# A hybrid attention block: the mixed values of two query tiles share one PSUM bank

## The chip, the cores and the metric

The kernel runs on one core of a Trainium2 chip. The core has a matrix engine (TensorE, PE in the profile), a vector engine (VectorE, DVE), a scalar engine (ScalarE, ACT), GpSimd (POOL), and queues that issue transfers (SyncE, SP). The metric is the device time of one execution in microseconds, as the median of several runs. The kernel before took 745.53 us (743.57 to 746.62, three runs).

## The reference

One encoder block on 1024 tokens of width 1024. The normalised input is projected once, and the parts feed attention, a gated spatial mix and the merge gates. Cut to what matters here:

```
q, k, v, gate_a, u_in, v_in, gate_b, g_merge = split(rmsnorm(x) @ w_in)
q, k = rope(rmsnorm(q)), rope(rmsnorm(k))      # 8 query heads, 2 key heads, 64 wide
p = softmax(q @ k.T / 8)                       # one row of 1024 weights per query
attn = (p @ v) * silu(gate_a)
gm = gelu(u_in) * v_mix * silu(gate_b)         # v_mix: spatial mix of layernorm(gelu(v_in))
y = sigmoid(g0) * (attn @ w_proj_attn) + sigmoid(g1) * (gm @ w_proj_gmlp)
out = rmsnorm(x + y @ w_out)
```

## The kernel before

Numbers that need more precision than the matrix engine's fast type gives are split into a high and a low part, and three products of parts make one product (`mm3`, L171). After the projections of k, v and q the kernel is in its attention stage, the part that the change edits.

**Scores.** Attention runs over 64 "heads": 4 groups `j` of two query heads, 8 query tiles `qt` of 128 tokens, 2 heads `h`; head number n is 16j + 2qt + h. For each, `scores` (L545) makes four matmuls of 512 columns into one of three PSUM tiles of 1024 columns (L550, L551), DVE takes the negated row maximum (`nm`, L553), ACT the exponential (`P`, L557), DVE the reciprocal of the sum (`ri`, L560), ACT the high part of the 16-bit weights (`p`, L563) and DVE their low part (L564). SP issues a transposing transfer of both parts (L567) into `T`, of which there are two buffers, one per pair (j, qt). Of `P` and `p` there are two buffers each for heads up to 11, and three from head 12 on.

**Mix.** `mix` (L569) multiplies the transposed weights of both heads of a pair (j, qt) with the values `vS`: 16 matmuls of 256 columns into the first half of the one PSUM bank `o`. The values' high parts sit in output partitions 0 to 63 and their low parts in 64 to 127, so ACT copies partitions 64 to 127 to SBUF (L578, tile `o2`, its own buffer) and DVE adds it to the other half, once for each head, 128 columns each (L582), into `og`. There are 32 mixes.

**Fills.** Between the heads stand 24 half projections of 512 tokens, the "fills": `u` (gelu), `gb` and `ga` (silu). Each is 24 matmuls of 512 columns (`z_mm`, L485) into the one PSUM bank `z`, which DVE evicts with a multiplication (`uw` L511, `gb..w` and `ga..w` L494), followed by two or three more steps on DVE and ACT and a product on POOL or DVE. Their SBUF tiles come from one set of four rotating tiles of 512 columns, `t2`. Their weights are loaded by SP into four raw buffers (`wraw`, L120), the high part is made by ACT (`wh`, L110) and the low part by POOL (`wl`, L116), which sets the raw buffer free.

**Order.** The text writes five scores ahead, two fills as a ramp, and then for each of 32 steps two more scores, one mix and the fills that `plan` gives to that step (L584 to L620). This is only where the tiles are handed out; a scheduler of the framework then sets the order of instructions on each engine, by its own model of time, and may place an instruction ahead of others of the text when its tiles are free. On the chip each engine takes its instructions strictly in that order.

**After it.** `proj_b` (L631, eight times 24 matmuls, `yb`) overlaps the stage's end, ACT and DVE make the sums and parts of the input that the gate products need (`xf`, `xfT`, `gf`, `gk`), and the gate products (`g`, L686 on) begin. Each gate weight is scaled by a factor (`scg`) from its squares: ACT squares four blocks of it (`gsq`, L814), PE adds them over the partitions (`usg`, L669), DVE and POOL make the factor, and ACT scales the weight (`wg`, L680).

Of the kernel before, what the change touches and what calls it, by code (L numbers as in the profile page):

```python
# [9 lines left out]
F32 = mybir.dt.float32  # L10
# [3 lines left out]
ALU = mybir.AluOpType  # L14
# [16 lines left out]
def hybrid_block_kernel(  # L31
# [11 lines left out]
    act, dve, pool, pe = nc.scalar, nc.vector, nc.gpsimd, nc.tensor  # L43

    sb = ctx.enter_context(tc.tile_pool(name="sb", bufs=1))
# [7 lines left out]
    def t4(tag, name, dt=F32, shape=(P, 1024)):  # L53
        return sb.tile(list(shape), dt, tag=tag, bufs=BUFS[tag], name=name)

    def t2(name, dt=F32):
        return sb.tile([P, 512], dt, tag="t2", bufs=4, name=name)

    def t8(tag, bufs, name, dt=F32R):
        return sb.tile([P, 2, 1024], dt, tag=tag, bufs=bufs, name=name)  # L60
# [13 lines left out]
    def ps_o(name):  # L74
        return ps.tile([P, 512], F32, tag="o", bufs=1, name=name)
# [7 lines left out]
    def H(h):  # L83
        return slice(512 * h, 512 * h + 512)

    def C(c):
        return slice(128 * c, 128 * c + 128)

    def heads(ap):
        return ap.rearrange("p (h d) -> p h d", d=64)  # L90
# [87 lines left out]
    for i in range(4):  # L178
        for j in range(2):
# [12 lines left out]
            for tt in range(NT):  # L192
                o = kvb[tt // 2][:, 256 * (tt % 2):256 * (tt % 2) + 256]
# [69 lines left out]
    for h in range(2):  # L263
        pt = ps_o(f"wsum{h}")
        pe.matmul(pt, ones, wsr[h], start=True, stop=True)
        for t in (2 * h, 2 * h + 1):
            for g2 in range(2):
                rows = slice(64 * g2, 64 * g2 + 64)
                dve.scalar_tensor_tensor(
                    out=bterm[rows, t, :], in0=pt[rows, C(2 * (t % 2) + g2)], scalar=cs[rows, C_LNB + t:C_LNB + t + 1],  # L270
                    in1=bsp[rows, C(t)], op0=ALU.mult, op1=ALU.add)
# [117 lines left out]
    for tab, o in (((rtk[:, 1, H(0)], rtk[:, 1, H(1)]), 128), (tabq, 0)):  # L389
        for half in range(2):  # L390
            dve.tensor_tensor(
                out=heads(tab[half]), in0=heads(rtk[:, 0, H(half)]),
                in1=gq[:, None, o + 64 * half:o + 64 * half + 64].broadcast_to([P, 8, 64]),
                op=ALU.mult)
# [5 lines left out]
    vS = sb.tile([P, 8, 2, 128], F16, tag="vS", bufs=1, name="vS")  # L400
# [19 lines left out]
                      in1=e2[:, None, :].broadcast_to([P, 2, 64]), op=ALU.mult)  # L420
# [57 lines left out]
    for t in range(4):  # L478
        m3 = vm[:, t, :].rearrange("p (c i) -> p c i", i=128)
        dve.scalar_tensor_tensor(out=m3, in0=m3, scalar=cs[:, C_LNG + t:C_LNG + t + 1],  # L480
                                 in1=bterm[:, t:t + 1, :].broadcast_to([P, 8, 128]),
# [40 lines left out]
    og, gat = {}, {}  # L522
# [45 lines left out]

    def mix(j, qt):  # L569
        v = j // 2  # L570
        ot = ps_o(f"o{j}{qt}")
        T = T16[j, qt]
        for kt in range(8):
            for p in range(2):
                pe.matmul(ot[:, 0:256], vS[:, kt, v, :], T[:, :, 8 * p + kt, :],  # L575
                          start=(kt == 0 and p == 0), stop=(kt == 7 and p == 1))
        o2 = sb.tile([64, 256], F32, tag="o2", bufs=1, name=f"o2{j}{qt}")
        act.copy(o2, ot[64:128, 0:256])  # L578
        if qt == 0:
            og[j] = t4("og", f"og{j}")  # L580
        for h in range(2):
            dve.tensor_tensor(out=og[j][64 * h:64 * h + 64, C(qt)], in0=ot[0:64, C(h)], in1=o2[:, C(h)], op=ALU.add)  # L582

    order = ["u2", "a0", "u0", "b1", "u1", "u3", "a1", "b0", "b2", "b3", "a2", "a3"]  # L584
    halves = [(o[0], int(o[1]), h) for o in order for h in range(2)]
    ramp = 2
# [25 lines left out]
    for n in range(32):  # L612
        if ramp + n in late:
            q_post(late[ramp + n], qsts[late[ramp + n]])
        for m in (2 * n + ahead, 2 * n + ahead + 1):
            if m < 64:
                scores(*hs[m])
        mix(*hs[2 * n][:2])
        for f in plan.get(n, []):
            run_fill(*f)  # L620
# [160 lines left out]
    for dt in range(8):  # L781
        proj_b(dt)
        if dt in XCS:
            j = XCS.index(dt)
# [97 lines left out]
    for step in MORDER.split():  # L882
# [13 lines left out]
        elif step[0] == "a":  # L896
            t = t8("qT", 4, f"ya{i}", F32)
# [135 lines left out]
```

## Time and profile before

| | |
|---|---|
| median of 3 runs | 745.53 us (743.57 to 746.62) |
| the profiled execution | 744.79 us |
| its span, first to last instruction | 743.0 us |
| mean granted TensorE clock | 0.988 |
| busy: PE, DVE, ACT, POOL | 712.1, 596.4, 446.8, 97.2 us |
| attention stage, mixes from first to last | 164 to 441 us |

A group of the profile names a line, an engine, the operation, what it writes and reads, the shapes, and the number of instructions; then the busy time and the mean duration of one in ns; then how long the engine stood idle just before them, and what ended most of that wait. A timeline row gives the start, the duration, and the idle time before it in brackets. Durations of neighbouring instructions overlap, so the price of one on a full engine is read from start to start.

### The profile page before, as it was taken

How to read it: one execution, taken by the hardware profiler on the slowest of the kernel's cores; microseconds unless marked ns; L12 is line 12 of the kernel's file. 1: busy time of each engine (PE TensorE's matmuls, PEld its weight loads, DVE VectorE, ACT ScalarE, POOL GpSimd, SP SyncE). 2: the span in 40 equal slices, each digit the busy share in tenths (PEclk: the TensorE clock that was granted, in tenths of full speed). 3: DMA queues.
4: the chain of work that ended last, by engine and by line, in shares of the span. 5: the costliest groups of instructions: out<-in, count | busy, mean ns of one | idle time of the engine just before them, and what ended most of it. 6: DMA issues, size and time to landing. Idle time of an engine off the chain costs nothing.

```text
span 743.0 us, 9814 instructions
## 1 busy us (share of the span) xinstructions
PE 712.1 (96%) x3561; PEld 530.1 (71%) x3561; DVE 596.4 (80%) x931; ACT 446.8 (60%) x775; POOL 97.2 (13%) x77
## 2 busy tenths in 40 slices
PE   8999999988999999999999995999999998999995
PEld 8978888766778888888878882455464555588884
DVE  5568988789798999988899999899888899934223
ACT  6646664676788898768787488555474446611101
POOL 0010242142121321232200002000000000000000
PEclk9999999989999999999999998999999999999998
DMA  8831301083769897898999800130031006241111
GB/s 309 301 100 36 114 15 42 1 142 78 136 128 181 166 179 142 162 177 157 166 234 323 183 16 1 56 128 15 18 125 57 0 1 231 109 142 68 46 58 56
DMA packets 152609, 85.47 MB, mean 115 GB/s; under 512 B 135408, under 2 KB 136048, under 8 KB 152560
## 3 DMA queue, kind: packets, MB, share of 16 engines
q1 hardware_dynamic: 152272, 84.56, 45.7%
q8 instruction: 28, 0.46, 0.3%
q10 hardware_dynamic: 288, 0.28, 0.1%
q14 instruction: 21, 0.17, 0.1%
HBM read 47.07 MB, written 4.19 MB: 69 GB/s over the span
## 4 chain that ended last, share of the span: by engine, by line
PE 81%; DVE 9%; DMA 4%; ACT 2%; issue 2%; POOL 1%; SPq 0%; POOLq 0%; DVEq 0%; ACTq 0%
PE o L575 6%; PE out L174 4%; PE out L173 4%; PE out L172 4%; DMA T<-p 3%; PE s L550 3%; PE s L551 3%; PE g L172 3%; PE g L174 3%; PE g L173 3%; PE q L172 2%; PE q L174 2%; PE v L172 2%; PE q L173 2%; PE v L173 2%; PE v L174 2%
## 5 line engine op out<-in xcount | busy, mean ns | idle before, releaser
L564 DVE SCALAR_TENSOR_TENSOR p<-P,ri,p 128x1024 f16<-128x1024 f32 x64 | 88.9, 1393 | 14.7 <-ACT p L563 14.3
L557 ACT ACTIVATE P<-s,nm 128x1024 f32<-128x1024 f32 x64 | 71.4, 1116 | 23.0 <-DVE nm L553 11.5
L553 DVE TENSOR_REDUCE nm<-s 128x1 f32<-128x1024 f32 x64 | 77.8, 1215 | 5.7 <-PE s L551 5.4
L563 ACT ACTIVATE p<-P,ri 128x1024 f16<-128x1024 f32 x64 | 72.8, 1143 | 14.7 <-DMA T<-p 11.3
L575 PE MATMUL o<-T,vS 128*128 128x256 f16 x512 | 61.8, 273 | 2.1 <-DMA T<-p 2.1
L575 PEld LDWEIGHTS <-vS 128*128 128x128 f16 x512 | 47.4, 98 | 16.0 <-issue 6.9
L550 PE MATMUL s<-kT,qT 128*128 128x512 f32 x128 | 53.0, 414 | 1.3 <-ACT P L557 1.3
L116 POOL TENSOR_TENSOR wl<-wraw,wh 128x512 fp32r<-128x512 f32 x24 | 36.0, 1504 | 111.6 <-ACT wh L110 96.2
L551 PE MATMUL s<-kT,qT 128*128 128x512 f32 x128 | 50.5, 395 | 0.0
L909 ACT ACTIVATE sq<-xr 128x1024 f32<-128x1024 f32 x7 | 7.4, 1061 | 61.5 <-DVE xr L963 61.5
L963 DVE TENSOR_TENSOR xr<-out,xr 128x1024 f32<-128x1024 f32 x7 | 8.6, 1225 | 44.0 <-PE out L174 43.9
L673 POOL TENSOR_TENSOR scg<-scg,mhalf 128x1 f32<-128x1 f32 x8 | 9.8, 1219 | 221.6 <-DVE scg L672 221.6
L110 ACT CAST wh<-wraw 128x512 fp32r<-128x512 f32 x35 | 21.5, 614 | 17.5 <-PE yb L173 7.5
L488 PE MATMUL ga<-xh,wh 128*128 128x512 f32 x64 | 26.5, 414 | 3.8 <-DVE uw L511 3.4
L550 PEld LDWEIGHTS s<-kT,qT 128*128 128x128 f32 x128 | 24.1, 188 | 6.7 <-ACT P L557 1.9
L551 PEld LDWEIGHTS s<-kT,qT 128*128 128x128 f32 x128 | 24.1, 188 | 4.9 <-issue 0.2
L488 PE MATMUL u<-xh,wh 128*128 128x512 f32 x64 | 25.6, 399 | 0.7 <-DVE ga01w L494 0.7
L490 PE MATMUL ga<-xh,wl 128*128 128x512 f32 x64 | 26.1, 407 | 0.0
L489 PE MATMUL ga<-xl,wh 128*128 128x512 f32 x64 | 26.0, 406 | 0.0
L680 ACT ACTIVATE wg<-graw,scg 128x512 f16<-128x512 f32 x16 | 11.4, 721 | 24.2 <-PE g L174 12.8
L172 PE MATMUL v<-nh,xh 128*128 128x512 f32 x64 | 25.5, 398 | 0.0
L174 PE MATMUL yb<-gmh,wl 128*128 128x512 f32 x64 | 25.5, 398 | 0.0
(557 smaller groups left out, 2158.5 us busy)
## 6 DMA issues: line engine op xcount, KB each, us to landing
wraw<-in_wall_dram SPq DMA_DIRECT2D x59, 256.0 KB, 3.2
graw<-in_wall_dram SPq DMA_DIRECT2D x16, 512.0 KB, 4.4
xraw<-in_xT_dram SPq DMA_DIRECT2D x15, 512.0 KB, 7.3
xn<-in_x_dram SPq DMA_DIRECT2D x8, 512.0 KB, 7.6
wor<-in_wall_dram SPq DMA_DIRECT2D x8, 512.0 KB, 4.9
xr<-in_x_dram SPq DMA_DIRECT2D x8, 512.0 KB, 5.1
out_dram<-xr SPq DMA_DIRECT2D x7, 512.0 KB, 2.6
T<-p SPq DMA_TRANSPOSE x64, 4.6
```

Source lines behind the costliest of these rows:

```text
L116: eng_lo.tensor_tensor(out=lo, in0=raw, in1=hi if hi.dtype == F16 else hi.bitcast(F32), op=ALU.subtract)
L172: pe.matmul(o, ah, bh, start=start, stop=False)
L173: pe.matmul(o, ah, bl, start=False, stop=False)
L174: pe.matmul(o, al, bh, start=False, stop=stop)
L488: pe.matmul(o, wh[:, C(dt % 4)], xh[dt][:, H(h)], start=(dt == 0), stop=False)
L550: pe.matmul(sp[:, H(hf)], qs, kT[:, 2 * v, H(hf)], start=True, stop=False)
L551: pe.matmul(sp[:, H(hf)], qs, kT[:, 2 * v + 1, H(hf)], start=False, stop=True)
L553: dve.tensor_reduce(out=nm, in_=sp, axis=AX.X, op=ALU.max, negate=True)
L557: act.activation(Pt, sp, AF.Exp, bias=nm, accum_out=rsum)
L563: act.activation(hi, Pt, AF.Copy, scale=ri)
L564: dve.scalar_tensor_tensor(out=lo, in0=Pt, scalar=ri, in1=hi, op0=ALU.mult, op1=ALU.subtract)
L575: pe.matmul(ot[:, 0:256], vS[:, kt, v, :], T[:, :, 8 * p + kt, :], start=(kt == 0 and p == 0), stop=(kt == 7 and p == 1))
```

## The change

The mixes of an even query tile and the odd one behind it share the bank: the even one writes columns 0 to 255, the odd one 256 to 511. Only after the odd one are they evicted, by one copy of 512 columns on ACT and two additions of 256 columns on DVE (two pieces of 128, picked by a stepped access), where two copies of 256 and four additions of 128 were. The copy's target is now one of the `t2` tiles that the fills use; the buffer `o2` is gone.

```
     def mix(j, qt):
         v = j // 2
-        ot = ps_o(f"o{j}{qt}")
+        if qt % 2 == 0:
+            ots[j] = ps_o(f"o{j}{qt}")
+        ot = ots[j][:, 256 * (qt % 2):256 * (qt % 2) + 256]
         T = T16[j, qt]
         for kt in range(8):
             for p in range(2):
-                pe.matmul(ot[:, 0:256], vS[:, kt, v, :], T[:, :, 8 * p + kt, :],
+                pe.matmul(ot, vS[:, kt, v, :], T[:, :, 8 * p + kt, :],
                           start=(kt == 0 and p == 0), stop=(kt == 7 and p == 1))
-        o2 = sb.tile([64, 256], F32, tag="o2", bufs=1, name=f"o2{j}{qt}")
-        act.copy(o2, ot[64:128, 0:256])
         if qt == 0:
             og[j] = t4("og", f"og{j}")
+        if qt % 2 == 0:
+            return
+        o2 = t2(f"o2{j}{qt}")[0:64, :]
+        act.copy(o2, ots[j][64:128, :])
+        o4, l4 = (t.rearrange("p (k h t) -> p k h t", k=2, h=2) for t in (ots[j], o2))
         for h in range(2):
-            dve.tensor_tensor(out=og[j][64 * h:64 * h + 64, C(qt)], in0=ot[0:64, C(h)], in1=o2[:, C(h)], op=ALU.add)
+            dve.tensor_tensor(
+                out=og[j][64 * h:64 * h + 64, 128 * qt - 128:128 * qt + 128].rearrange("p (k t) -> p k t", k=2),
+                in0=o4[0:64, :, h, :], in1=l4[:, :, h, :], op=ALU.add)
+    ots = {}
```

The line numbers behind this function grow by 8 in the changed kernel. The scheduler sets a new order on every engine from the first mixes on. Three places of it follow.

DVE before, around the eviction of the second `gb` half (gb11w). `p` is a head's low part, `nm` its maximum, `ri` its reciprocal, `og` a mix's two additions.

```order
L582 TENSOR_TENSOR og_1659<-o_2012,o_2029 64x128 x2
L560 RECIPROCAL ri_1987<-ri_1987 128x1
L564 SCALAR_TENSOR_TENSOR p_1951<-P_1945,ri_1948,p_1951 128x1024
L553 TENSOR_REDUCE nm_2038<-s_2033 128x1
L564 SCALAR_TENSOR_TENSOR p_1990<-P_1984,ri_1987,p_1990 128x1024
L560 RECIPROCAL ri_2004<-ri_2004 128x1
L494 TENSOR_TENSOR gb11w<-gb_2297,rB 128x512
L553 TENSOR_REDUCE nm_2055<-s_2050 128x1
L560 RECIPROCAL ri_2043<-ri_2043 128x1
L564 SCALAR_TENSOR_TENSOR p_2007<-P_2001,ri_2004,p_2007 128x1024
```

The same eviction on DVE in the changed kernel, with what follows it.

```order
L553 TENSOR_REDUCE nm_2703<-s_2698 128x1
L560 RECIPROCAL ri_2673<-ri_2673 128x1
L494 TENSOR_TENSOR gb11w<-gb_2277,rB 128x512
L564 SCALAR_TENSOR_TENSOR p_2676<-P_2670,ri_2673,p_2676 128x1024
L497 SCALAR_TENSOR_TENSOR gb11t<-gb11t,gb11w 128x512
L511 TENSOR_TENSOR uw_2398<-u_2373,rB 128x512
L275 SCALAR_TENSOR_TENSOR ut_2400<-ut_2400,uw_2398 128x512
L587 TENSOR_TENSOR og_2360<-o_2343,o_2457 64x256 x2
L277 SCALAR_TENSOR_TENSOR ut_2400<-ut_2400,uw_2398 128x512
L511 TENSOR_TENSOR uw_2538<-u_2513,rB 128x512
L275 SCALAR_TENSOR_TENSOR ut_2540<-ut_2540,uw_2538 128x512
```

Before, gb11w stood among heads 14 to 18 (`nm_2055` is head 18's maximum); now it stands behind head 31's maximum (`nm_2703`), and two of the four halves of u1 and u3 follow with hardly a head between them.

SP before, from the transposes of pair 10 (heads 20 and 21) to those of pair 12; `wraw` is a weight's load.

```order
L567 DMA_TRANSPOSE T_2122<-p_2119 128x16x128
L120 DMA wraw_3126<-in_wall_dram 128x512
L567 DMA_TRANSPOSE T_2122<-p_2341 128x16x128
L120 DMA wraw_3362<-in_wall_dram 128x512
L567 DMA_TRANSPOSE T_2361<-p_2358 128x16x128
L567 DMA_TRANSPOSE T_2361<-p_2443 128x16x128
L567 DMA_TRANSPOSE T_2463<-p_2460 128x16x128
L567 DMA_TRANSPOSE T_2463<-p_2499 128x16x128
```

SP in the changed kernel, the same pairs.

```order
L567 DMA_TRANSPOSE T_2103<-p_2100 128x16x128
L567 DMA_TRANSPOSE T_2103<-p_2321 128x16x128
L567 DMA_TRANSPOSE T_2341<-p_2338 128x16x128
L567 DMA_TRANSPOSE T_2341<-p_2419 128x16x128
L120 DMA wraw_2607<-in_wall_dram 128x512
L120 DMA wraw_2838<-in_wall_dram 128x512
L120 DMA wraw_2844<-in_wall_dram 128x512
L120 DMA wraw_3075<-in_wall_dram 128x512
L120 DMA wraw_3081<-in_wall_dram 128x512
L567 DMA_TRANSPOSE T_2439<-p_2436 128x16x128
L567 DMA_TRANSPOSE T_2439<-p_2474 128x16x128
```

Before, loads stood between single transposes; now five stand in a row ahead of the transposes of pair 12 (`T_2439`, heads 24 and 25).

ACT before, at the end of the stage, from the copy of the last `proj_b` product to the first scaled gate weight.

```order
L637 COPY y_4201<-yb_4546 128x1024
L110 CAST gk<-gat_3889 128x1024
L814 ACTIVATE gsq_4733,gss_4732<-graw_4729 128x512
L110 CAST gf_4914<-gat_3889 128x1024
L110 CAST xfT_4268<-xraw_4208 128x512
L814 ACTIVATE gsq_4735,gss_4732<-graw_4729 128x512
L814 ACTIVATE gsq_4737,gss_4732<-graw_4729 128x512
L814 ACTIVATE gsq_4739,gss_4732<-graw_4729 128x512
L110 CAST xfT_4314<-xraw_4210 128x512
L680 ACTIVATE wg_4606<-graw_4578,scg_4592 128x512
```

ACT in the changed kernel, the same stretch.

```order
L645 COPY y_4121<-yb_4466 128x1024
L110 CAST gk<-gat_3820 128x1024
L110 CAST xfT_4241<-xraw_4130 128x512
L110 CAST xfT_4423<-xraw_4253 128x512
L110 CAST gf_4834<-gat_3820 128x1024
L110 CAST xfT_4241<-xraw_4132 128x512
L688 ACTIVATE wg_4526<-graw_4498,scg_4512 128x512
```

The four squares (`gsq`) that stood behind the copy have moved ahead of it.

## The prediction

> **What bounds the kernel now.** First the page: the busy shares, then the engines' shares of the chain that ended last.
>
> ```profile
> PE 712.1 (96%) x3561; PEld 530.1 (71%) x3561; DVE 596.4 (80%) x931; ACT 446.8 (60%) x775; POOL 97.2 (13%) x77
> PE 81%; DVE 9%; DMA 4%; ACT 2%; issue 2%; POOL 1%; SPq 0%; POOLq 0%; DVEq 0%; ACTq 0%
> ```
>
> TensorE (PE) carries 81% of the chain, but busy time alone does not say that it is full, since its rows overlap. So next the stretches of time. The attention stage, which the change edits, runs from 164 to 441 us; after it come the gap before the gate products (441 to 456) and the rest.
>
> ```profile
> 164.00:240.00 76.00, 71.23 (x400) 57.28 (x399) 66.13 (x94) 56.85 (x108) 17.95 (x12) 1.00 0.71 131
> 240.00:280.00 40.00, 40.00 (x215) 32.43 (x213) 39.77 (x57) 34.86 (x63) 11.29 (x8) 1.00 0.91 177
> 280.00:441.00 161.00, 159.75 (x845) 128.86 (x844) 145.79 (x217) 118.65 (x204) 22.38 (x15) 1.00 0.83 178
> 441.00:456.00 15.00, 7.37 (x33) 5.64 (x32) 14.50 (x26) 14.70 (x31) 1.54 (x1) 0.88 0.00 1
> ```
>
> The columns are start:end, length, then busy us of PE, weight loads, DVE, ACT and POOL, the clock, the DMA share and GB/s. Two engines are full at once: PE pauses for 6 us in 277, and DVE reaches 39.77 of 40 us between 240 and 280. Between 441 and 456 PE stands for half of the time.
>
> How far PE really is from its limit is read from start to start, in a stretch of its timeline without idle time (18 matmuls of 512 columns, one mix of 16 matmuls of 256, then scores):
>
> ```profile
> 359.66 0.40 PE L488 MATMUL ga<-xh,wh 128*128 128x512 f32 x1
> ...
> 363.58 0.40 PE L551 MATMUL s<-kT,qT 128*128 128x512 f32 x1
> 363.82 1.92 PE L575 MATMUL o<-T,vS 128*128 128x256 f16 x16
> 365.49 0.48 PE L550 MATMUL s<-kT,qT 128*128 128x512 f32 x1
> 365.81 0.39 PE L551 MATMUL s<-kT,qT 128*128 128x512 f32 x1
> ```
>
> 18 starts in 4.16 us are 0.231 us each, and I use 0.2325; a mix takes 1.67 us and 0.09 more at the change of type, 1.76 us or 0.11 per matmul. The DVE's prices from start to start, in the same way, stand in these rows (maximum, a mix's two additions, a silu step, a weight's low part, a reciprocal, a head's low part; then an addition of 256 columns):
>
> ```profile
> 395.56 1.22 DVE L553 TENSOR_REDUCE nm<-s 128x1 f32<-128x1024 f32 x1
> 396.70 0.57 DVE L582 TENSOR_TENSOR og<-o,o 64x128 f32<-64x128 f32 x2
> 397.30 0.69 DVE L497 SCALAR_TENSOR_TENSOR ga30t<-ga30t,ga30w 128x512 f32<-128x512 f32 x1
> 397.91 0.68 DVE L116 TENSOR_TENSOR wl<-wraw,wh 128x512 fp32r<-128x512 f32 x1
> 398.51 0.15 DVE L560 RECIPROCAL ri<-ri 128x1 f32<-128x1 f32 x1
> 398.58 1.26 DVE L564 SCALAR_TENSOR_TENSOR p<-P,ri,p 128x1024 f16<-128x1024 f32 x1
> 399.77 0.68 DVE L494 TENSOR_TENSOR ga31w<-ga,rB 128x512 f32<-128x512 f32 x1
> ...
> 488.55 0.40 DVE L714 TENSOR_TENSOR ps<-wraw 128x256 f32<-128x256 f32 x1
> 488.87 0.68 DVE L696 TENSOR_TENSOR gb<-g1T,ga 128x512 f32<-128x512 f32 x1
> ```
>
> That is 1.14, 0.60 (two of 0.30), 0.61, 0.60, 0.07, 1.19, and 0.32 for 256 columns.
>
> **The direct saving.** The copies and additions, by form, with a 512-wide cast beside them:
>
> ```profile
> L582 DVE TENSOR_TENSOR og<-o,o 64x128 f32<-64x128 f32 x64 | 17.8, 278 | 1.7 <-ACT o L578 1.2
> L578 ACT COPY o<-o 64x256 f32<-64x256 f32 x32 | 11.9, 371 | 9.1 <-PE o L575 8.4
> L110 ACT CAST wh<-wraw 128x512 fp32r<-128x512 f32 x27 | 16.6, 613 | 12.4 <-PE yb L173 7.5 <-PE u L489 1.6 <-issue 1.4
> ```
>
> Sixteen pairs of mixes each lose two additions. On DVE a pair costs 4 x 0.30 = 1.20 us now and 2 x 0.33 = 0.66 after: 16 x 0.54 = 8.6 us. That row of 256 columns reads SBUF and the new additions read PSUM in steps; at worst two cost what four did, at best the same 0.32. On ACT two copies of 0.371 become one of about 0.61: 16 x 0.13 = 2.1 us. The Trainium skill (Perfetto Trace Analysis, Optimizing Scalar/DVE Operations) gives a fixed access overhead of about 125 ns for DVE and 51 ns for ScalarE on PSUM; by it 32 fewer additions would save an estimated 4.0 us and 16 fewer copies 0.8 us. The rows give twice that on DVE; with either, the sum below is the same but for 1 us, since only eight additions fall in the stretch that decides.
>
> None of this shortens the stage by itself. PE has the same rows, 0.2325 and 0.11 us each, and fills the stage.
>
> **What moves.** The copy's target is no longer a tile of its own but one of the four rotating 512-column tiles (t2) that the fills use too. These are handed out in the order of the text. A fill whose text stands behind a mix can no longer be placed before that mix's copy. Before, the scheduler ran fills ahead: the first u half after the ramp was evicted (uw_2213) behind head 8's low part. In the new order it is evicted (uw_2193) only behind head 19's. Attention then runs for a while with few fills, and four u halves follow in a heap.
>
> In the part before the heap PE has little to do per head and DVE much. I sum both from fixed points, the end of head 5's score matmuls at 167.00 us on PE and head 4's low part at 168.34 on DVE, to the eviction of gb11 (gb11w), which frees the only z bank for the first u half of the heap.
>
> ```profile
> 167.00 0.83 PE L575 MATMUL o<-T,vS 128*128 128x256 f16 x6
> 168.34 1.28 DVE L564 SCALAR_TENSOR_TENSOR p<-P,ri,p 128x1024 f16<-128x1024 f32 x1
> 225.29 0.67 DVE L494 TENSOR_TENSOR gb11w<-gb,rB 128x512 f32<-128x512 f32 x1
> L564 DVE SCALAR_TENSOR_TENSOR p<-P,ri,p 128x1024 f16<-128x1024 f32 x60 | 83.2, 1390 | 14.7 <-ACT p L563 14.3
> ...
> 175.23 2.53 DVE L326 TENSOR_TENSOR qtmp<-qst,tabq 128x256 f32<-128x256 f32 x4
> 178.95 1.20 DVE L329 TENSOR_TENSOR qst<-qst,tabq 128x1024 f32<-128x1024 f32 x1
> 180.07 0.57 DVE L582 TENSOR_TENSOR og<-o,o 64x128 f32<-64x128 f32 x2
> ```
>
> A head's low part averages 1.39 us where a single row shows 1.28, so I price it at 1.19 + 0.11 = 1.30. DVE in the new order, up to gb11w: 26 maxima x 1.14 = 29.6; 26 reciprocals x 0.075 = 2.0; 24 low parts x 1.30 = 31.2; 8 additions x 0.33 = 2.6; 16 steps of 512 x 0.62 = 9.9; the last q group's rope, four of 0.63 (2.53 in the row) and three of 1.13, 5.9; together 81 us, so 249.5 at the earliest. PE by then has 227 matmuls of 512, 150 of 256 and 24 transposes of 128, under 0.11 each and 1.8 in all: 52.8 + 16.5 + 1.8 = 71.1, and eight score matmuls behind gb11 (1.9): 167.0 + 73.0 = 240.0. It must wait.
>
> How much longer than 81 us DVE takes is the unknown, x. Below: heads up to number 11 share two buffers of the transposed weights, and a buffer's round is ACT's 1.14, DVE's 1.28 and the transpose:
>
> ```profile
> L563 ACT ACTIVATE p<-P,ri 128x1024 f16<-128x1024 f32 x60 | 68.2, 1142 | 14.7 <-DMA T<-p 11.3 <-DVE ri L560 3.2
> T<-p SPq DMA_TRANSPOSE x64, 4.6
> ```
>
> 7.0 us for two heads, 3.5 each: from head 6 (DVE sum 12.8, so 181.1) to head 12 six times, 202.1, where the DVE sum says 200.1. So x is 2 at least. Above: in the kernel before, DVE's 71 rows to gb11w sum to 49 us and took 225.29 - 168.34 = 57, 8 us or 16% in waits; 14% of 81 is 11. Between 240 and 280 DVE waited for 0.5%, so it can run tight when it has a backlog. I take x = 6: gb11w at 255.5, its 0.65, first u matmul at 256.2. PE has then waited 256.2 - 240.0 = 16.2 us, and about 0.9 more at the turn from the first to the second u half, where nothing else stands between: last matmul's end and one eviction of 0.60. In the rest of the stage I give 1.5 (0 to 4) for mixes that wait for transposes. Waits after: 18.6. Before: PE's rows from 167.0 to the end of the last proj_b matmul sum to 273.5 in both orders; they ended at 447.1, so 6.6 us were waits. The end of the stage moves by +12.0, to 459.1.
>
> **What comes back at the end of the stage.** Before, PE stood here:
>
> ```profile
> 446.90 0.40 PE L174 MATMUL yb<-gmh,wl 128*128 128x512 f32 x1
> 448.43 0.39 PE L669 MATMUL usg<-gss,mhalf 128*128 128x4 f32 x2 [1.14 <-ACT gsq L814]
> 454.48 0.59 PE L669 MATMUL usg<-gss,mhalf 128*128 128x4 f32 x2 [5.67 <-ACT gsq L814]
> 455.90 0.61 PE L172 MATMUL g<-xf,wg 128*128 128x512 f16 x1 [0.82 <-ACT wg L680]
> ...
> L637 ACT COPY y<-yb 128x1024 f32<-128x1024 f32 x6 | 6.1, 1013 | 2.7 <-DMA T<-p 2.6
> L110 ACT CAST gmh<-vm 128x1024 fp32r<-128x1024 f32 x4 | 3.9, 1042 | 0.0
> ```
>
> 8.8 us from 447.1 to the first gate product, on ACT's squares of the gate weights (gsq). In the new order all eight squares stand ahead of the copy of the last proj_b product. Behind that copy ACT has, before the first scaled gate weight, the copy itself (1.0), two casts of 1024 columns (1.04 each), three of 512 (0.61 each) and the weight (0.6): 5.5 us. At best these are done early and only the scale's own steps are left, which I bound by 454.48 to 455.90 and the power on POOL, 3.1. I take 5.5: first gate product at 464.6, against 455.9. **+8.7 us**; DVE's 8.6 us less work lets it keep up there and is worth nothing beyond it.
>
> The profiled execution took 744.79 us (span 743.0 and 1.8 around it), 0.7 below the median of 745.53. So 753.5 in the profile's terms, about 754.0 as a median. Ends: x = 2, no late waits, 3.1: +0.8, so 746.3; x = 11, 4 us of late waits, 5.5: +16.2, so 761.7.
>
> **Rivals.**
>
> No change (within 0.5%, 3.7 us, about what a measurement of this kernel can tell). Place: the gap of 8.8 us after the stage. If DVE runs the early stretch with x of 3 or less, PE ends the stage 7 to 9 us late, the gap shrinks to 3.1 to 5, and PE's lateness is nearly paid back: 745 to 748. It decides at gb11w: by 252 us or not. For: DVE's 0.5% between 240 and 280. Against: 16% of waits in the same stretch before, and ACT's row above, which waited 11.3 us for transposes.
>
> Slower by more: the transposes wait behind weight loads.
>
> ```profile
> 228.74 15.16 SPq L567 DMA_TRANSPOSE T<-p  x5
> ```
>
> A transpose holds SP's queue for 3.0 us when five follow each other. In the new order five loads stand ahead of head 24's transpose; the fifth needs the raw buffer that POOL frees with the low part of the u3 weights, behind ACT's cast, behind the first heaped u half. From gb11w: 0.7 and 24 x 0.2325 = 5.6 for that half, five steps of 0.6 for its gelu and the cast, two POOL steps of 1.4 (11.29 us for 8 between 240 and 280), 1 for the load: 13.1. Head 25's transpose starts 3.0 later and lands 4.6 after that, at 20.7; PE reaches its mix after three u halves, one turn and two mixes, 0.7 + 16.8 + 0.9 + 3.5 = 21.9. One microsecond of margin: if ACT does two heads first (four rows of about 1.14), PE waits 3.4 us there, and about as much at the next mixes: 757 to 762.
>
> Slower by the bank: two mixes wait for one eviction. The Trainium skill (Perfetto Trace Analysis, Matmuls) says that independent groups should rotate through PSUM banks, so that one's eviction overlaps the next's matmuls; here one bank serves both. As a mechanism of this kernel: a copy of 0.61 and two additions of 0.66, 1.3 us at each of 15 boundaries, +19 us, if PE had nothing else. For it: nothing in the trace; before, the same bank was handed over 31 times, and the idle time ahead of the mixes, 2.1 us in the row below, names transposes alone. Against: at the heap's boundary 5.6 us of u matmuls stand between, elsewhere scores or a fill.
>
> ```profile
> L575 PE MATMUL o<-T,vS 128*128 128x256 f16 x512 | 61.8, 273 | 2.1 <-DMA T<-p 2.1
> ```
>
> Faster: DVE, not PE, set the pace from 240 to 456, and its 8.6 us show. It needs x below 1 and PE's waits at 441 to 456 gone: 740. PE's 40.00 of 40 speaks against it.
>
> **How the numbers follow.** Forecast (749 to 758) 0.46; no change 0.25; late transposes 0.17; the bank 0.06; faster 0.06. Slower by over 0.5% is 0.46 + 0.17 + 0.06 = 0.69, within it 0.25, faster 0.06. The range leaves out the faster case, most of the bank's and the worst of the transposes: 744.5 to 764.
>
> **What would show it.** In the profile after: gb11w at about 255 us where it was 225; some 16 us of PE idle time between 167 and 257, released by DVE; four u halves nearly back to back behind it; the last proj_b matmul at about 459; the gap to the first gate product down from 8.8 to about 5; the additions at about 0.41 us each and the copies at 0.61. The argument is wrong if PE shows no more idle time before 260 than the 6 us of before, or if the stage ends by 450, or if PE's new idle time names the copy or the additions.

## The result and the profile after

The changed kernel takes 762.66 us (median of 4 runs, 762.38 to 762.86) where the kernel before took 745.9 us beside it (743.57 to 746.62): a ratio of 1.0225, 95% interval 1.0208 to 1.0243. It is slower by 16.8 us, where the prediction said 8.5. The profiled execution took 762.86 us, with a span of 761.1 us. First the busy line of its page.

```profile
PE 717.6 (94%) x3561; PEld 531.8 (70%) x3561; DVE 590.0 (78%) x899; ACT 445.6 (59%) x759; POOL 92.9 (12%) x77
```

DVE and ACT have the fewer instructions that the change promised (899 for 931, 759 for 775), and less to do. PE has as many as before, yet is busy for 5.5 us longer. The stretches of time, with the columns of the prediction, show where.

```profile
164.00:240.00 76.00, 61.72 (x336) 47.36 (x334) 64.55 (x88) 58.83 (x108) 7.18 (x5) 0.89 0.76 141
240.00:280.00 40.00, 38.94 (x191) 31.25 (x190) 25.80 (x37) 22.79 (x40) 15.80 (x12) 1.00 0.39 76
280.00:441.00 161.00, 158.05 (x852) 127.63 (x851) 139.18 (x189) 118.46 (x196) 27.46 (x19) 1.00 0.92 194
...
456.00:474.00 18.00, 9.76 (x45) 7.83 (x43) 17.11 (x30) 10.21 (x16) 4.47 (x2) 0.85 0.00 0
```

Between 164 and 240 us PE gets through 336 matmul rows instead of 400, and its clock is 0.89 instead of 1.00. Between 240 and 280 it is nearly full (38.94 of 40 us), but DVE, which was full there before, has 25.80 us of work in 40: the four u halves that stand in a heap give it little to do. After 280 the two kernels look alike. So most of the loss arises before 240, and a second, smaller part at the end. The early one on PE's timeline, with the idle time in brackets:

```profile
175.43 0.79 PE L550 MATMUL s<-kT,qT 128*128 128x512 f32 x1 [2.27 <-ACT P L557]
183.49 0.54 PE L349 MATMUL qtp<-identr,qs 128*128 128x128 f32 x4 [2.65 <-ACT P L557]
185.15 0.63 PE L349 MATMUL qtp<-identr,qs 128*128 128x128 f32 x4 [1.12 <-ACT qT L351]
190.11 3.60 PE L577 MATMUL o<-T,vS 128*128 128x256 f16 x16 [4.33 <-DMA T<-p]
209.86 1.92 PE L577 MATMUL o<-T,vS 128*128 128x256 f16 x16 [0.68 <-DMA T<-p]
214.82 0.50 PE L550 MATMUL s<-kT,qT 128*128 128x512 f32 x1 [2.10 <-ACT P L557]
216.72 3.28 PE L577 MATMUL o<-T,vS 128*128 128x256 f16 x16 [0.69 <-DMA T<-p]
222.29 1.92 PE L577 MATMUL o<-T,vS 128*128 128x256 f16 x16 [0.43 <-DMA T<-p]
...
261.24 0.39 PE L488 MATMUL u<-xh,wh 128*128 128x512 f32 x1
```

The brackets sum to 14.3 us, all before 223 us; they name the exponential that frees a score tile (`P`), the transposes, and the last query tiles. From 222.29 to the first u matmul of the heap at 261.24 PE shows no more gap. And two mixes took 3.60 and 3.28 us, where the same 16 matmuls take 1.92: in the slices from 190 to 200 and from 210 to 220 us the granted clock was 0.72 and 0.83.

The end of the stage, on PE, on DVE, on GpSimd (POOL) and on ACT:

```profile
464.90 0.39 PE L174 MATMUL yb<-gmh,wl 128*128 128x512 f32 x1
...
474.18 0.61 PE L172 MATMUL g<-xf,wg 128*128 128x512 f16 x1 [7.93 <-ACT wg L688]
```

```profile
469.19 0.15 DVE L680 TENSOR_SCALAR scg<-scg 128x1 f32<-128x1 f32 x1
...
473.40 0.16 DVE L682 RECIPROCAL scg<-scg 128x1 f32<-128x1 f32 x1 [0.38 <-POOL scg L681]
```

```profile
L681 POOL TENSOR_TENSOR scg<-scg,mhalf x8: 548/549/3943, 469.4 to 623.3; 128x1 f32<-128x1 f32 x8
```

```profile
473.40 1.33 ACT L688 ACTIVATE wg<-graw,scg 128x512 f16<-128x512 f32 x2 [3.62 <-POOL scg L681]
```

The last proj_b matmul starts at 464.90 (446.90 before), the first gate product at 474.18 (455.90 before): +18.0 and +18.3 us. The gap between them did not shrink. The third row gives the eight powers of the gate weights' scales, as least, median and greatest duration in ns: 549 is usual, the first took 3943, and the first weight (`wg`) waited for it. Behind the first gate product nothing changed: 761.1 - 474.18 = 286.9 us are left, and 743.0 - 455.9 = 287.1 before.

The edited operations themselves, by form, and on DVE's timeline:

```profile
L587 DVE TENSOR_TENSOR og<-o,o 64x256 f32<-64x256 f32 x32 | 13.2, 413 | 2.1 <-ACT o L584 1.9
L584 ACT COPY o<-o 64x512 f32<-64x512 f32 x16 | 9.4, 585 | 4.4 <-PE o L577 4.0
```

```profile
370.45 0.84 DVE L587 TENSOR_TENSOR og<-o,o 64x256 f32<-64x256 f32 x2
371.31 0.16 DVE L560 RECIPROCAL ri<-ri 128x1 f32<-128x1 f32 x1
```

DVE's additions fell from 17.8 to 13.2 us of busy time, ACT's copies from 11.9 to 9.4. From start to start two additions take 0.86 us, where four took 1.20.

### The profile page after: what moved, and what is told of

Same layout as the page of the kernel before. It is cut to its first block, busy times and chain, and to the rows that moved or that the text cites. A ratio compares the mean times of both kernels' runs of the same rounds, so it can differ in the third digit from the quotient of the medians.

```text
span 761.1 us, 9743 instructions
## 1 busy us (share of the span) xinstructions
PE 717.6 (94%) x3561; PEld 531.8 (70%) x3561; DVE 590.0 (78%) x899; ACT 445.6 (59%) x759; POOL 92.9 (12%) x77
## 5 line engine op out<-in xcount | busy, mean ns | idle before, releaser
L564 DVE SCALAR_TENSOR_TENSOR p<-P,ri,p 128x1024 f16<-128x1024 f32 x64 | 87.0, 1359 | 24.1 <-ACT p L563 23.6
L577 PE MATMUL o<-T,vS 128*128 128x256 f16 x512 | 65.7, 283 | 6.5 <-DMA T<-p 6.5
L577 PEld LDWEIGHTS <-vS 128*128 128x128 f16 x512 | 49.0, 101 | 23.2 <-issue 8.1
L550 PE MATMUL s<-kT,qT 128*128 128x512 f32 x128 | 54.0, 422 | 4.6 <-ACT P L557 4.6
L551 PE MATMUL s<-kT,qT 128*128 128x512 f32 x128 | 51.5, 402 | 0.0
L116 POOL TENSOR_TENSOR wl<-wraw,wh 128x512 fp32r<-128x512 f32 x24 | 37.8, 1575 | 104.3 <-ACT wh L110 79.4
L681 POOL TENSOR_TENSOR scg<-scg,mhalf 128x1 f32<-128x1 f32 x8 | 7.8, 974 | 216.4 <-DVE scg L680 146.6
L174 PE MATMUL v<-nh,xl 128*128 128x512 f32 x64 | 25.4, 396 | 0.0
```

Source lines behind the costliest of these rows:

```text
L116: eng_lo.tensor_tensor(out=lo, in0=raw, in1=hi if hi.dtype == F16 else hi.bitcast(F32), op=ALU.subtract)
L174: pe.matmul(o, al, bh, start=False, stop=stop)
L550: pe.matmul(sp[:, H(hf)], qs, kT[:, 2 * v, H(hf)], start=True, stop=False)
L551: pe.matmul(sp[:, H(hf)], qs, kT[:, 2 * v + 1, H(hf)], start=False, stop=True)
L564: dve.scalar_tensor_tensor(out=lo, in0=Pt, scalar=ri, in1=hi, op0=ALU.mult, op1=ALU.subtract)
L577: pe.matmul(ot, vS[:, kt, v, :], T[:, :, 8 * p + kt, :], start=(kt == 0 and p == 0), stop=(kt == 7 and p == 1))
```

## The experiments

The theory T: the time is lost because the copy's target comes out of t2. Its tiles are handed out in the order of the text, so each fill hangs on the mixes that stand ahead of it, and the scheduler's new order leaves PE without fills early. The rivals: the shared bank costs by its hand-over (B), or the wide copy and the stepped additions do (W). Four kernels tell these apart, on one chip, beside 745.37 us for the kernel before.

**The shared bank with a buffer of its own.** One line of the changed kernel:

```
-        o2 = t2(f"o2{j}{qt}")[0:64, :]
+        o2 = sb.tile([64, 512], BF16, tag="o2", bufs=1, name=f"o2{j}{qt}")
```

> The changed kernel with one thing undone: the copy's target is again a buffer of its own, 64x512 in 16 bits (1 KB, what the old one took), instead of a t2 tile. The bank is still shared and the copy and the additions are still wide; the order has the first u half behind the ramp (u0) at head 10 again instead of head 22. Theory T (the time is lost because the fills hang on the mixes through t2): 740 to 748 us, no heap, gb11w evicted by about 225 us. Rival B (the shared bank itself costs, by its hand-over): about 762 us. Rival W (the wide copy or the stepped additions cost): about 762 us too, told from B by the next kernel.

Measured: 743.27 us, ratio 0.997 (0.996 to 0.998). The first two stretches of its profile:

```profile
164.00:240.00 76.00, 73.93 (x403) 60.15 (x403) 65.15 (x89) 55.66 (x106) 23.67 (x14) 0.99 0.68 130
240.00:280.00 40.00, 38.90 (x218) 30.91 (x217) 37.87 (x50) 32.75 (x57) 7.77 (x7) 1.00 0.93 177
```

PE has its 403 rows between 164 and 240 us again, at a clock of 0.99, and DVE has work behind 240. The bank is shared exactly as in the change. gb11w is evicted at 220.23 us. All of the loss goes with the one buffer, as T says. B falls, and W too as far as this kernel goes: its copy writes 16-bit numbers, so it is not quite the operation of the change. The last of these four kernels has the change's own copy and additions.

**The t2 tile alone.** One line of the kernel before:

```
-        o2 = sb.tile([64, 256], F32, tag="o2", bufs=1, name=f"o2{j}{qt}")
+        o2 = t2(f"o2{j}{qt}")[0:64, 0:256]
```

> The kernel before with one part of the change alone: the copy's target (256 columns) is a t2 tile; every mix keeps the bank for itself and its own copy and two additions. T: slower than before by at least half of the change's loss, 755 to 765 us, with u0 at head 22 in the order and gb11w at 250 us or later. B and W: 746 us, as before, since nothing is shared or wide.

Measured: 777.48 us, ratio 1.0423 (1.040 to 1.0447). Slower, as T says, and by 32 us, twice the change's loss and beyond what was expected. PE's longest waits from 167 to 482 us:

```profile
PE s L550 <- ACT P L557: 12.9, 12, 3.3
PE o L575 <- DVE og L582: 3.3, 3, 2.2
PE o L575 <- DMA T<-p: 3.2, 3, 1.6
```

The columns are what waited for what: us in total, times, longest. Here all 32 mixes take a t2 tile instead of 16. PE waits for score tiles twelve times, over the whole stage, and mixes wait for the additions of the one before. So it is not the pairing that loses the time: with it, and with half as many copies in t2, the loss is half of this one.

**Shared bank, narrow operations.** In the changed kernel, behind the odd mix:

```
         for k in range(2):
             o2 = sb.tile([64, 256], F32, tag="o2", bufs=1, name=f"o2{j}{qt}{k}")
             act.copy(o2, ots[j][64:128, 256 * k:256 * k + 256])
             for h in range(2):
                 dve.tensor_tensor(out=og[j][64 * h:64 * h + 64, C(qt - 1 + k)],
                                   in0=ots[j][0:64, 256 * k + 128 * h:256 * k + 128 * h + 128], in1=o2[:, C(h)], op=ALU.add)
```

> Shared bank, evicted behind the odd mix, but with two copies of 256 and four additions of 128 and the old buffer of 256 columns. T: 743 to 749 us, DVE busy about 8 us more than with the wide additions, and that without effect on the time, as PE fills the stage. B: about 762 us. W: 746 us here and 762 us with the wide operations.

Measured: 742.14 us, ratio 0.9959 (0.9945 to 0.9972). Beside the wide operations (743.27 us, 0.996 to 0.998) it is not slower, and DVE is busy for 594.3 us instead of 590.1. So the wide operations save DVE 4.2 us, and no time of the kernel is seen from them. The two differ in their orders as well, so this is not exact: the last proj_b matmul ended at 446.0 us here and at 447.2 with the wide operations, and the gap behind it was 10.3 us here and 7.0 there.

**The t2 tile with fills handed out earlier.** In the changed kernel:

```
-    order = ["u2", "a0", "u0", "b1", "u1", "u3", "a1", ...
+    order = ["u2", "u0", "b1", "a0", "u1", "u3", "a1", ...
```

The `ga` fills may not stand ahead of the mixes whose result they multiply, and the list keeps its sequence. So a0 held back u0 and b1 in the text, behind eight mixes.

> The changed kernel, t2 tile and all, with the list of fills in another sequence: u0 and b1 are handed out ahead of a0, so that they stand ahead of the first mixes' copies in the text. In the order they are back at heads 5 to 10, and u1 and u3 are no heap but lie between heads 22 and 34. T: 742 to 752 us, most of the 17 us comes back although the copy still takes a t2 tile. If the t2 tile costs in itself, by fills that wait on the chip for a tile that a copy holds: 755 us or more.

Measured: 745.37 us, ratio 0.9997 (0.9988 to 1.0007). The copy still takes a t2 tile, wide and from a shared bank, and the 17 us are gone; gb11w is evicted at 203.9 us. W falls for good. It is not the tile that costs on the chip, but the place of the fills in the text ahead of or behind it. What this list would do to the kernel before was not tried.

Two terms of the sum were still open, the slow rows and the gap at the end. Four more kernels, beside 745.59 us for the kernel before.

**Early mixes done twice.** In the changed kernel:

```
+        for _ in range(2 if j == 0 and qt < 5 else 1):
             for kt in range(8):
                 for p in range(2):
                     pe.matmul(ot, vS[:, kt, v, :], T[:, :, 8 * p + kt, :],
```

> The changed kernel with the 16 matmuls of each of the first five mixes done twice into the same columns (the second pass overwrites the first, so the output is unchanged): 5 x 1.76 = 8.8 us more work for TensorE, in the stretch where it idles and its granted clock falls to 0.72 to 0.83. The order elsewhere is that of the changed kernel. Theory K (TensorE's slow clock behind its idle time lengthens the chain from head to head, and this is the 4 to 6 us by which gb11w came later than the price of DVE's rows and the forecast waits say): the clock stays nearer to 1, gb11w at 257 us or earlier in spite of the added work, 757 to 761 us. Rival (the clock is only a symptom; the transposes and two weight buffers set the pace): gb11w at 260 us or later, 763 to 770 us.

Measured: 761.01 us, ratio 1.0218 (1.019 to 1.0246); the change's own ratio of 1.0225 lies inside. First the changed kernel from 168.3 to 220 us, then this one.

```profile
168.30:180.00 11.70, 9.43 (x54) 7.06 (x53) 10.35 (x17) 7.45 (x16) 0.34 (x1) 0.85 0.47 90
180.00:190.00 10.00, 2.00 (x12) 1.19 (x10) 8.05 (x10) 7.20 (x15) 0.00 (x0) 0.77 0.56 105
190.00:200.00 10.00, 9.89 (x45) 7.91 (x46) 6.97 (x11) 6.79 (x15) 0.00 (x0) 0.72 0.70 134
200.00:210.00 10.00, 9.32 (x50) 6.79 (x49) 7.27 (x11) 8.26 (x16) 1.67 (x2) 1.00 0.51 106
210.00:220.00 10.00, 7.20 (x41) 5.11 (x40) 9.87 (x13) 8.55 (x16) 0.89 (x1) 0.83 1.04 201
```

```profile
168.30:180.00 11.70, 10.74 (x74) 8.39 (x72) 10.36 (x17) 7.72 (x17) 0.38 (x1) 1.00 0.48 90
180.00:190.00 10.00, 7.07 (x49) 5.17 (x48) 8.02 (x10) 7.67 (x16) 0.00 (x0) 0.89 0.70 107
190.00:200.00 10.00, 10.00 (x61) 8.11 (x60) 8.02 (x13) 9.02 (x17) 0.00 (x0) 0.93 0.66 125
200.00:210.00 10.00, 9.09 (x59) 7.22 (x58) 8.36 (x11) 6.96 (x13) 2.38 (x1) 1.00 0.80 128
210.00:220.00 10.00, 7.99 (x51) 5.91 (x49) 8.99 (x13) 8.87 (x16) 1.28 (x1) 1.00 1.08 217
```

The column behind POOL's is the granted clock. PE's busy time times the share of the clock that is missing is an estimate of how much longer the slow rows took: 9.43 x 0.15 + 2.00 x 0.23 + 9.89 x 0.28 + 7.20 x 0.17 = 5.9 us in the changed kernel, and 7.07 x 0.11 + 10.00 x 0.07 = 1.5 us here. With 8.8 us more work for PE the stage was not longer but a little shorter: in the trace gb11w came at 257.81 us (259.57) and the last proj_b matmul at 463.99 (464.90). The rival, which expected gb11w at 260 us or later, falls by its own number. But K is not shown by this run. It expected gb11w at 257 us or earlier, and the total cannot be told from the changed kernel's. The added work also filled idle time: PE's brackets up to 223 us sum to 7.2 us here, 7.1 less than before the edit, and the estimate for the slow rows fell by 4.4. Nor did the order stay that of the changed kernel: DVE's first two additions stand at 174.05 us there, ahead of three steps of the rope, and at 177.70 us here, behind two of them. So this run does not part the clock from the idle time.

**The scale without the power.** In the changed kernel; `absw` holds a constant, so that the matmul over the partitions already gives the inverse of the scale:

```
-            act.activation(junk(f"gsq{dt}{i}"), t, AF.Square, accum_out=ss[:, i:i + 1])
+            act.activation(junk(f"gsq{dt}{i}"), t, AF.Abs, accum_out=ss[:, i:i + 1])
...
-        pe.matmul(pt[:, 0:n], mhalf[:, 0:1].broadcast_to([P, P]), ss, start=True, stop=True)
+        pe.matmul(pt[:, 0:n], absw.broadcast_to([P, P]), ss, start=True, stop=True)
...
-        dve.tensor_scalar(out=sc[:, 0:1], in0=sc[:, 0:1], scalar1=-(2.0 ** -27), scalar2=1e-30, ...
-        pool.tensor_tensor(out=sc[:, 0:1], in0=sc[:, 0:1], in1=mhalf[:, 0:1], op=ALU.pow)
-        dve.reciprocal(sc[:, 1:2], sc[:, 0:1])
+        dve.reciprocal(sc[:, 0:1], sc[:, 1:2])
```

> The changed kernel with the gate weights' scale taken from sums of absolute values in place of squares (the scale only brings the weights into the 16-bit range and is divided out again), so that GpSimd's power falls away and a reciprocal on DVE stands where the scaling of the sum stood. Theory G (the gap at the stage's end is the power on GpSimd, which took 3.94 us there against 0.55 where DVE is idle): gap of about 5 us instead of 9.05, 758 to 759.5 us. Rival (DVE, late by its forms, sets the gap whatever the power takes): 761.5 to 763 us.

Measured: 760.62 us, ratio 1.0214 (1.0188 to 1.0241). The stage's end in its timeline on PE, and the reciprocal on DVE:

```profile
465.39 0.39 PE L176 MATMUL yb<-gmh,wl 128*128 128x512 f32 x1
...
470.95 0.52 PE L174 MATMUL g<-xf,wg 128*128 128x512 f16 x1 [4.22 <-ACT wg L688]
```

```profile
469.69 0.16 DVE L682 RECIPROCAL scg<-scg 128x1 f32<-128x1 f32 x1
```

The gap is 470.95 - 465.62 = 5.3 us instead of 9.05, with DVE as late as before: its reciprocal stands at 469.69 where the scaling of the sum stood at 469.19. So it was the power, as G says. Of the 3.7 us the span keeps 2.3: the stage ended 0.5 us later, and 0.9 us were lost behind the first gate product. The total lies between what the two theories expected, and its interval does not part it from the changed kernel; the gap decides.

The same profile says something on the clock. Up to the scale's steps every engine has the order of the changed kernel, but the slow rows lay elsewhere. PE's timeline, to be laid beside the rows of the changed kernel at 175.43, 216.72, 222.29 and 261.24:

```profile
177.18 0.52 PE L552 MATMUL s<-kT,qT 128*128 128x512 f32 x1 [2.27 <-ACT P L559]
...
217.16 1.91 PE L579 MATMUL o<-T,vS 128*128 128x256 f16 x16 [0.65 <-DMA T<-p]
...
222.77 1.92 PE L579 MATMUL o<-T,vS 128*128 128x256 f16 x16 [0.99 <-DMA T<-p]
...
261.80 0.39 PE L490 MATMUL u<-xh,wh 128*128 128x512 f32 x1
```

It came to the first wait 1.75 us later and to the heap 0.56 us later, so it made good 1.2 us on the way. The estimate of above, with the same slices, gives 9.25 x 0.11 + 3.95 x 0.16 + 8.13 x 0.23 = 3.5 us for its slow rows, 2.4 less than in the changed kernel. So about half of the difference came through. The mix at 217.16 took 1.91 us and not 3.28, and that gained nothing: PE then waited for an exponential and for the next transposes, and the next mix started at 222.77 instead of 222.29.

**Both repairs together, and the measure for it.** The narrow kernel above and the kernel before, each with the same edit of the scale.

> Shared bank, own narrow buffer, narrow copies and additions (742.1 us when it ran above), with the scale without the power. By G: the 3.3 us beyond the 0.55 of an undisturbed power fall away, and the scaling's own row: 737 to 739.5 us. By the rival: 741 to 743 us.

> The kernel before with the scale without the power, as the measure for the run ahead: there the power took only 1.54 us and the squares ended 0.8 us ahead of it. G: 743 to 745 us. If the absolute values or the other order gain by themselves: 741 us or less.

Measured: 740.70 us, ratio 0.9934 (0.9915 to 0.9954), and 744.93 us, ratio 0.9992 (0.9979 to 1.0004). The gap of the first:

```profile
443.39 0.40 PE L176 MATMUL yb<-gmh,wl 128*128 128x512 f32 x1
...
450.36 0.61 PE L174 MATMUL g<-xf,wg 128*128 128x512 f16 x1 [4.53 <-ACT wg L687]
```

It beats both kernels of this case, at 6.7 us of gap; without the edit its gap was 10.3 (446.0 to 456.30 us). The 740.70 us lie above the 737 to 739.5 that G expected, and its interval overlaps that of the narrow kernel with the power (0.9945 to 0.9972). In the kernel before the edit does nothing, since ACT's squares end the gap there (PE waits 5.67 us for them), as expected.

## Why the prediction was right in kind and short in size

**The direct saving.** Worth nothing, as predicted, and shown by the wide and the narrow kernel side by side, as far as two orders can be compared. Its size on DVE was too high: an addition of 256 columns was priced at 0.33 us, and it takes 0.43 from start to start. So a pair saves 1.20 - 0.86 = 0.34 us, 5.4 in all and not 8.6. The estimate of 4.0 us that the prediction drew from the Trainium skill (Perfetto Trace Analysis, Optimizing Scalar/DVE Operations) agrees with the trace's 17.8 - 13.2 = 4.6 us of busy time. ACT saved 2.5 us where 2.1 were forecast and the same section gave 0.8.

**The cause.** Right: the t2 tile and the order of the text, shown from both sides, by leaving it out of the change and by putting it alone into the kernel before.

**The early stretch.** The step that failed is the wait at gb11w. The prediction added up PE's rows and DVE's rows apart, let PE run ahead to 240.0 us, and let it wait there for DVE, 16.2 us long. The trace has no such wait:

```profile
259.57 0.69 DVE L494 TENSOR_TENSOR gb11w<-gb,rB 128x512 f32<-128x512 f32 x1 [0.19 <-PE gb L490]
...
266.91 0.69 DVE L511 TENSOR_TENSOR uw<-u,rB 128x512 f32<-128x512 f32 x1 [3.83 <-PE u L490]
```

There DVE waited for PE. PE could not run ahead. It had run dry 37 to 86 us earlier, head by head, at the score tiles and the transposes, 14.3 us in all, and from 222 us on its remaining work was the bound, with no gap up to the heap. So PE's early waits add to its rows, where the prediction took the later of two sums. x, the excess over the 81 us of DVE's rows, came to 10.2 us (259.57 - 168.34 - 81) and not 6. The waits of DVE in the same stretch before had given 11 as its upper end (16% of 81 would be 13; the 14% are a share of the time with the waits in it); the value was taken lower because of the 0.5% of a stretch in which DVE had a backlog.

A second term was put at nothing: PE's rows were priced at 0.2325 and 0.11 us each, "on a full engine", in a stretch where PE was forecast to idle. Up to the heap, 240.0 as worked out, 14.3 of waits and the estimated 5.9 of slow rows make 260.2; it began at 261.24. One us stays unexplained. The 5.9 is how much longer the rows took, and not what the full clock would have saved: where two profiles of one order can be laid side by side, 1.2 of 2.4 us came through. How much of the 5.0 us by which the heap came late is the clock's, and how much the chain from head to head, stays open.

That the waits sum up as forecast is luck. Forecast were 16.2 + 0.9 + 1.5 = 18.6 us, and the trace's list of PE's waits from 167 to 466 us is this:

```profile
PE o L577 <- DMA T<-p: 6.5, 5, 4.3
PE s L550 <- ACT P L557: 4.6, 3, 2.3
PE qtp L349 <- ACT P L557: 2.7, 1, 2.7
PE u L488 <- DVE uw L511: 1.9, 2, 1.1
PE ga L488 <- DVE ga30w L494: 1.5, 1, 1.5
PE qtp L349 <- ACT qT L351: 1.1, 1, 1.1
```

That is 18.3 us, but none of it at gb11w. And with the same waits the stage ended at 465.1 and not at 459.1, 6.0 us later.

**The turn in the heap.** Forecast 0.9 us for the turn from the first half to the second. PE's two waits for `uw` in the list above are 0.8 us there and 1.1 at the turn to the last half: small, as forecast.

**The gap.** Forecast 5.5 us from ACT's list; measured 9.05. The list was right: without the power the gap is 5.3. What was mis-sized is the scale's own steps, bounded by 3.1 us from a place in the kernel before where the power took 1.54 us. Here it took 3.94. So the pay-back of 3.3 us did not come. The kernel before shows such a power too, its second one, behind the first gate product, which the bound left aside:

```profile
460.40 4.54 POOL L673 TENSOR_TENSOR scg<-scg,mhalf 128x1 f32<-128x1 f32 x1 [5.32 <-DVE scg L672]
```

Together: 5.0 us at the heap's first matmul (261.24 for 256.2), 1.0 more to the stage's end, 3.5 at the gap. With the forecast of 8.7 these make 18.2 of the 18.3 us.

**The rivals.** The bank: refuted, since the kernels that share it with a buffer of their own are as fast as before. "No change" decided at gb11w by 252 us, and it came at 259.57. The late transposes were real but cost PE next to nothing. SP's queue, and the mix of pair 12:

```profile
247.15 26.42 SPq L120 DMA_DIRECT2D wraw<-in_wall_dram  x5
```

```profile
282.77 1.91 PE L577 MATMUL o<-T,vS 128*128 128x256 f16 x16 [0.36 <-DMA T<-p]
```

The five loads held SP's queue for 26 us, so no transpose started from 247 to 275. The next one started 15.6 us behind gb11w (275.20 - 259.57), where 13.1 were forecast; that sum had 1 us for a load, and the page of before gives a median of 3.2 us from issue to landing for `wraw`. ACT and DVE stood (DVE 14.2 us in 240 to 280), while PE, with four halves in a row, waited 0.36 us at that mix.

## What to carry to other kernels

Where a buffer set rotates in the order of the text, a new user of it is a dependency for every user behind it; look at where the scheduler then puts the large independent pieces of work, before counting saved instructions. A private buffer of the old size kept this edit local, and handing the independent work out earlier did the same without one. Two engines that are tied to each other item by item do not run ahead of each other: their waits come early and add to the rows, so the later of two sums is too short. Where a forecast lets TensorE idle, price its rows behind the idle time at the lower clock as well, as an upper end: in part the slow rows only take the place of waits.

## What the runs showed of the hardware

TensorE's clock fell behind short idle times: behind 2.1 to 4.3 us of them the granted clock in slices of some 10 us was 0.72 to 0.85, and a mix took 3.60 us instead of 1.92. The Trainium skill (TensorE: Matmul & The Clock Gate, Part 1: The HAM clock gate) says that the gate halves the clock after an idle window of about 3.4 us and needs a busy one to open again. 3.60 against 1.92 us is near that half; but here 2.10 us were enough once (at 214.82 in the changed kernel) and not another time (at 215.31 in the one without the power, where the next mix took 1.91 us). 8.8 us of repeated matmuls in that stretch did not lengthen the time: they filled idle time, and the clock in it was 0.89 or more.

A power of 128 numbers on GpSimd took 0.55 us as a rule. In the gap at the stage's end, where DVE adds and subtracts nearly without pause, it took 0.94 us (own buffer), 1.54 (before), 3.34 (narrow, and fills earlier) and 3.94 (changed). The Trainium skill (SBUF — State Buffer, SBUF: two separate sides) says that DVE and GpSimd share a pair of ports, which one instruction holds to its end, and names DVE's instructions with two SBUF inputs. The traces of this gap agree, and show more: the power did not get in between several such instructions in a row, and it ended about 0.5 us behind the first of DVE's instructions with fewer inputs from SBUF, or behind DVE's first pause. In the changed kernel that is a scaling of one column (at 472.86, the power's end at 473.36 us), with the own buffer a reduction that reads PSUM (452.87 and 453.37), in the kernel before a pause (from 454.67, the end at 455.09). This is read from the traces; no run moved such an instruction. Nor does it cover all: with the own buffer the second power ended at 457.12 us, behind the start of an instruction with two inputs from SBUF (456.60).
